# All expert score blocks from f32r parts, and 24 of them ahead of the combine loop instead of 14

## The chip, the cores and the metric

The kernel runs on one core of a Trainium2 chip. The metric is the time of one execution on the device in microseconds (us), from the profiler's first to its last event; of several runs the median counts. The engines are TensorE (PE, with its weight loads shown apart as PEld), VectorE (DVE), ScalarE (ACT), GpSimd (POOL) and SyncE (SP), which issues most of the DMAs. Each engine works through its own instructions in order.

## What is computed

The program is two layers of an encoder for 512 tokens of width 1024. A layer has two kinds of attention, an output projection with a LayerNorm, and then a retrieval over 16,384 single-neuron experts (PEER), which takes nearly all of the time spoken of here:

```python
def chunk(xc):
    q = (xc @ wq).reshape(PEER_CHUNK, PEER_HEADS, 2, half)
    sc = jnp.einsum('chpd,hpnd->chpn', q, sub_keys)
    ...
    eidx = jnp.take_along_axis(cidx, pos, axis=-1)
    g = jax.nn.softmax(top_s, axis=-1)
    u_sel = jnp.take(u, eidx, axis=0)
    a = jax.nn.gelu(jnp.einsum('chkd,cd->chk', u_sel, xc), approximate=False)
    w = (g * a).astype(x.dtype)
    v_sel = jnp.take(v, eidx, axis=0)
    return jnp.einsum('chk,chkd->cd', w, v_sel)
```

Each token picks 128 experts (8 heads of 16), takes the GELU of its product with their rows of `u`, weighs it with the gates `g`, and adds up their rows of `v`. Everything is in float32.

## The kernel before

The 512 tokens are four chunks of 128. Chunk 0 (`gat`) is done as the reference says it: its rows of `u` and `v` are gathered by indirect DMAs. Chunks 1 to 3 (`dense`, 384 tokens) are done densely: the 16,384 experts are 128 blocks (`NB`) of 128, all products of a block with the 384 tokens are computed, and the gates, which are zero for experts that a token did not pick, are laid out in a matrix `G` in DRAM.

A layer's retrieval runs through these stages, in the names of the code:

- `start(2)`, the queries and keys of chunk 0, with `top_pairs` and `gates` of chunk 3 beside it. `gates(c)` turns gates and expert indices of a chunk with TensorE and leaves them in flat tiles: `gh`, `glf`, `gl` (the gate's upper half, the rest, and the rest in f16) and `iT` (the two index halves).
- The tokens of the three dense chunks are turned by `transpose_rows` into `xTd`, a whole f32 copy; after the next stage two instructions (L908, L909) split it into `xTh` and `xTl`, its upper and lower part in the type f32r, on which TensorE multiplies at reduced precision.
- `spread()` builds `G` on chip, eight tokens at a time, 48 steps in all. A step has on DVE the one-hot masks `o12` (L873), the weighted masks `ah` (L874) and `al` (L875), on ACT two small instructions of `al` (L878) and two copies of the result into `stg` (L887), on TensorE 16 matmuls in f16 (L884, L885). Four steps fill a `stg` of 2 MB, which SP stores to `G`.
- `acts()` computes the expert blocks, `ge = gelu(u @ x)`. It is a generator, and a call `next(am)` makes one block. Of the first `LEAD` = 14 blocks each is 8 f32 matmuls on `xTd` (L826), which the hardware runs as two passes each. All later ones split the block's 1024 columns of `ut` into `uh` (ACT, L830) and `ul` (DVE, L831) and do 24 f32r matmuls (L833 to L835). During `spread()` one block is made every fourth step until there are 13; the 14th follows it.
- The combine loop runs over the 128 blocks. Iteration `blk` makes expert block `blk + LEAD`, splits a block of `v` into `vh`, `vl` (L1051, L1052), multiplies `ge` by the gates (`w`, L1055), splits that into `wh`, `wl` (L1058, L1059) and does 18 f32r matmuls of 512 columns (L1018 to L1020). Beside this, DVE does `jobs`, the 300 steps of chunk 0 (37 of ranking, 128 products with rows of `u`, 128 sums with rows of `v`, 7 at the end); 256 of them wait for a gather (L975) into one of four slots. The list `pace` says how the jobs are shared out: weight 4 for an iteration that still makes an expert block (`b < NB - LEAD`), 1 after that, 0 for the first and the last six.

A scheduler sets each engine's order from the program and a cost of its own. DVE in the combine loop is the exception (`manual_schedule`): there the order is that of the code. Pools lie in a stack on two sides of SBUF (`left`, `right`), so that a pool can only be made where an earlier one was released; `ws`, four buffers of 1 MB, holds `w_pq`, `ut` and `vt` in turn.

```python
        for i, _ in enumerate(spread()):
            if i % 4 == 0 and len(gel) < LEAD - 1:
                next(am)
        act.copy(xTh, xTd)
        v.tensor_tensor(out=xTl, in0=xTd, in1=xTh.bitcast(F32), op=SUB)
        while len(gel) < LEAD:
            next(am)
```

Of the kernel before, what the change touches and what calls it, by code (L numbers as in the profile page):

```python
# [34 lines left out]
GS = 2.0 ** 15  # L35
TG = 32
GB = 4
LEAD = 14
NTAIL = 6
NCAND = [TK // (a + 1) for a in range(TK)]  # L40
COFF = [sum(NCAND[:a]) for a in range(TK)]
# [4 lines left out]
def encoder_kernel(ctx: ExitStack, tc: tile.TileContext, x, ln_in_g, ln_in_b, w_in, qn_g, kn_g, sink,  # L46
# [18 lines left out]
    def sbuf(name, bufs=1, side="left"):  # L65
        return tc.alloc_tile_pool(name=name, bufs=bufs, side=side, reuse_waits="tile")
# [10 lines left out]
    h = cp.tile([P, NC, D], F32, name="h")  # L77
# [121 lines left out]
    for l in range(L):  # L199
        kp = sbuf(f"kp{l}", bufs=2, side="right")  # L200
# [86 lines left out]
        for c in gat + dense:  # L287
            cs = slice(c * P, (c + 1) * P)
# [7 lines left out]
            b = proj(c, wk, "ps_k")  # L296
# [470 lines left out]
        gp = sbuf(f"ge{l}")  # L767
        xp = sbuf(f"x{l}")
        lp = sbuf(f"lg{l}")
        xd = sbuf(f"xd{l}")  # L770
        ga = sbuf(f"ga{l}")
        flat = {}

        def gates(c):

            b = acc_bank("ps_t")
            i12 = ga.tile([P, 2, P], F32, tag="i12", name="i12", bufs=1)
            v.tensor_copy(i12[:, 0], i1f[:, c, :])
            v.tensor_copy(i12[:, 1], i2f[:, c, :])
            for i, src in enumerate((gte[:, c, :], i12[:, 0], i12[:, 1])):  # L780
                pe.transpose(b[:, i * P:(i + 1) * P], src, ident)
            gT = ga.tile([P, P], F32, tag="gT", name="gT", bufs=1)
            gh = ga.tile([P, P], F16, tag="gh", name="gh", bufs=3)
            glf = ga.tile([P, P], F32, tag="glf", name="glf", bufs=3)
            gl = ga.tile([P, P], F16, tag="gl", name="gl", bufs=3)
            iT = ga.tile([P, P // 8, 2, 8], F16, tag="iT", name="iT", bufs=3)
# [12 lines left out]
        gates(order[2])  # L799
        pt.release()  # L800
        tp.release()
        sp = sbuf(f"sp{l}", bufs=2, side="right")
        sp.tile([P, 8, P, 2], F16, tag="o12", name="o12")
        for tag in ("ah", "al"):
            sp.tile([P, 4, P, 2], F16, tag=tag, name=tag)
        xTd = xd.tile([P, KD, ND], F32, name="xTd")
        sp.tile([P, NB, TG], F32, tag="stg", name="stg", bufs=1)
        for ci, c in enumerate(dense):
            transpose_rows(h[:, c, :], xTd[:, :, ci * P:(ci + 1) * P], f"tr_x{c}")
        gg0 = xp.tile([P, NTG, GB, TG], F32, name="gg0")  # L810
        xTh = xp.tile([P, KD, ND], F32R, tag="xT", name="xTh", bufs=2)
        xTl = xp.tile([P, KD, ND], F32R, tag="xT", name="xTl", bufs=2)
        ff = "p k e -> p (k e)"
        gel = []

        def acts():

            for g2 in range(NB // 2):
                ut = load_w(peer_ut[l, g2], "ut")
                for bi in range(2):  # L820
                    us = ut[:, bi * D:(bi + 1) * D]
                    b = mm_bank("ps_a")
                    if len(gel) < LEAD:
                        u4 = us.rearrange("p (k e) -> p k e", k=KD)
                        for k in range(KD):
                            pe.matmul(b[:, :ND], u4[:, k, :], xTd[:, k, :], start=k == 0, stop=k == KD - 1)  # L826
                    else:
                        uh = up.tile([P, KD, P], F32R, tag="uh", name="uh")
                        ul = up.tile([P, KD, P], F32R, tag="ul", name="ul")
                        act.copy(uh.rearrange(ff), us)  # L830
                        v.tensor_tensor(out=ul.rearrange(ff), in0=us, in1=uh.rearrange(ff).bitcast(F32), op=SUB)  # L831
                        for k in range(KD):
                            pe.matmul(b[:, :ND], uh[:, k, :], xTh[:, k, :], start=k == 0, stop=False)  # L833
                            pe.matmul(b[:, :ND], uh[:, k, :], xTl[:, k, :], start=False, stop=False)  # L834
                            pe.matmul(b[:, :ND], ul[:, k, :], xTh[:, k, :], start=False, stop=k == KD - 1)  # L835
                    ge = gp.tile([P, ND], F32, tag="ge", name="ge", bufs=LEAD)
                    act.activation(ge, b[:, :ND], AF.Gelu)
                    gel.append(ge)
                    yield
# [62 lines left out]
                        keep(2 * GB, NB)  # L902

        am = acts()
        for i, _ in enumerate(spread()):
            if i % 4 == 0 and len(gel) < LEAD - 1:
                next(am)
        act.copy(xTh, xTd)  # L908
        v.tensor_tensor(out=xTl, in0=xTd, in1=xTh.bitcast(F32), op=SUB)  # L909
        while len(gel) < LEAD:  # L910
            next(am)


        ga.release()
        xd.release()
        sp.release()
        kp.release()
        up = sbuf(f"u{l}", bufs=2)
        ep = sbuf(f"ex{l}", bufs=2, side="right")
        ep.tile([P, D], F32R, tag="vh", name="vh")  # L920
        ep.tile([P, D], F32R, tag="vl", name="vl")
        ep.tile([P, NTG, TG], F32, tag="w", name="w")
        ep.tile([P, ND], F32R, tag="wh", name="wh")
        ep.tile([P, ND], F32R, tag="wl", name="wl")
        ep.tile([P, NTG, GB, TG], F32, tag="gg", name="gg")
# [100 lines left out]
        with tc.manual_schedule(engines={mybir.EngineType.DVE}):  # L1026
            for g2 in range(NB // 2):
                if g2 > 0:
                    load_v(g2)
                vt = vts[g2]  # L1030
                if g2 == 0:
                    gg = gg0
                elif (g2 * 2) % GB == 0:
                    gg = ep.tile([P, NTG, GB, TG], F32, tag="gg", name="gg")
                    load_g(gg, g2 * 2, 0, NTG)
                for bi in range(2):
                    blk = g2 * 2 + bi
                    if len(gel) < NB:
                        next(am)
                    turn = max(0, blk + LEAD - NB) % 3  # L1040
                    if turn == 1:
                        t = xp.tile([P, KD, ND], F32R, tag="xT", name="vwt", bufs=2).rearrange("p k n -> p (k n)")
                        vh, vl, wh, wl = t[:, :D], t[:, D:2 * D], t[:, 2 * D:2 * D + ND], t[:, 2 * D + ND:2 * (D + ND)]
                    else:
                        vp, tg_h, tg_l = (up, "uh", "ul") if turn else (ep, "vh", "vl")
                        vh = vp.tile([P, D], F32R, tag=tg_h, name="vh")
                        vl = vp.tile([P, D], F32R, tag=tg_l, name="vl")
                        wp, tg_h, tg_l, nb = (gp, "ge", "ge", LEAD) if turn else (ep, "wh", "wl", None)
                        wh = wp.tile([P, ND], F32R, tag=tg_h, name="wh", bufs=nb)
                        wl = wp.tile([P, ND], F32R, tag=tg_l, name="wl", bufs=nb)  # L1050
                    act.copy(vh, vt[:, bi, :])  # L1051
                    v.tensor_tensor(out=vl, in0=vt[:, bi, :], in1=vh.bitcast(F32), op=SUB)  # L1052
                    ge = gel[blk]
                    w_ = ep.tile([P, NTG, TG], F32, tag="w", name="w")
                    v.scalar_tensor_tensor(w_, gg[:, :, blk % GB, :], 1.0 / GS,  # L1055
                                           ge.rearrange("p (a t) -> p a t", a=NTG), op0=MUL, op1=MUL)
                    wf = w_.rearrange("p a t -> p (a t)")
                    act.copy(wh, wf)  # L1058
                    v.tensor_tensor(out=wl, in0=wf, in1=wh.bitcast(F32), op=SUB)  # L1059
                    if blk < NB - NTAIL:  # L1060
                        for c in dense:
                            for n in range(2):
                                combine(c, n, blk, wh, wl, vh, vl)
                    else:
                        parts.append((blk, wh, wl, vh, vl))
                    want = len(jobs) * sum(pace[:blk + 1]) // sum(pace)
                    while done < want:
                        f, j = jobs[done]
                        f(j)
                        done += 1  # L1070
# [81 lines left out]
```

## Time and profile before

| | |
|---|---|
| runs | 3059.69, 3058.49, 3059.13 us; median 3059.13 us |
| profiled execution | 3056.56 us, of which the span of the core's instructions is 3054.5 us |
| granted TensorE clock, mean | 0.996 of full speed |
| PE busy | 2980.2 us (98%) |
| DVE, ACT, POOL busy | 2420.0, 1333.8, 756.4 us |
| DMA | 749.44 MB, 245 GB/s in the mean |

The profile gives the busy time of each engine, its groups of instructions with what ended the idle time before them, the waits, the chain of work that ended last, and each instruction in order of time. The durations of matmuls are modelled and overlap; what a matmul costs is read from the distance of two starts. Below, layer 0 is read; layer 1 has the same stages about 1514 us later.

### The profile page before, as it was taken

Reading aid. Unit: us, or ns where it says so; the run is one execution under the profiler, and the core shown is the slowest. Engines: PE = TensorE matmul, PEld = TensorE weight load, DVE = VectorE, ACT = ScalarE, POOL = GpSimd, SP = SyncE. Lnnn points to the kernel's source line nnn. Section 1 sums busy time; section 2 is a strip of 40 time slices with the busy share of each in tenths; the row PEclk is TensorE's granted clock in tenths of the full one; section 3 lists DMA queues with packets and bytes.
Section 4 is the critical chain, followed back from the end, with each engine's and each line's share of the span. In section 5 each row is a group of like instructions: output and inputs, shape, how many; then the busy total and the mean of one; then the engine's idle time right before and its main releaser. Section 6 shows DMA issues by size and latency. Waiting matters only on the chain. (4 is left out here: it accounts for less than half of the span.)

```text
span 3054.5 us, 47487 instructions
## 1 busy us (share of the span) xinstructions
PE 2980.2 (98%) x17858; PEld 2696.5 (88%) x17858; DVE 2420.0 (79%) x5050; ACT 1333.8 (44%) x2646; POOL 756.4 (25%) x524
## 2 busy tenths in 40 slices
PE   7999999999999999999999999999999999999998
PEld 7999877999999999999898998779999999999997
DVE  7767998778777777877777779977788777777777
ACT  4664277343333333333347642764333333333332
POOL 0000000024434454454000000000344434455440
PEclk9999999999999999999999999999999999999999
DMA  5014767569889889889420247675698888988982
GB/s 195 27 58 148 242 241 289 194 226 332 324 306 327 320 302 332 313 310 327 165 97 15 72 150 268 247 297 174 248 330 306 321 325 304 325 322 304 327 312 90
DMA packets 262230, 749.44 MB, mean 245 GB/s; under 512 B 19952, under 2 KB 130288, under 8 KB 231792
## 3 DMA queue, kind: packets, MB, share of 16 engines
q1 hardware_dynamic: 188272, 477.94, 43.5%
q0 software_dynamic: 73728, 268.47, 24.5%
q8 instruction: 140, 2.29, 0.3%
q14 instruction: 90, 0.74, 0.1%
HBM read 691.81 MB, written 54.53 MB: 244 GB/s over the span
## 5 line engine op out<-in xcount | busy, mean ns | idle before, releaser
L975 POOL DMA_INDIRECT gt<-in_dram,idx x512 | 748.3, 1461 | 2042.5 <-DVE idx L966 1184.8
L833 PE MATMUL ps_a<-xTh,uh 128*128 128x384 f32 x1824 | 610.1, 334 | 3.7 <-ACT uh L830 3.7
L835 PE MATMUL ps_a<-xTh,ul 128*128 128x384 f32 x1824 | 610.1, 335 | 0.0
L834 PE MATMUL ps_a<-xTl,uh 128*128 128x384 f32 x1824 | 609.9, 334 | 0.0
L1020 PE MATMUL ff<-vh,wl 128*128 128x512 f32 x1476 | 575.8, 390 | 0.0
L1018 PE MATMUL ff<-vh,wh 128*128 128x512 f32 x1476 | 575.0, 390 | 0.1
L1019 PE MATMUL ff<-vl,wh 128*128 128x512 f32 x1476 | 573.8, 389 | 0.0
L1051 ACT CAST vh<-vt 128x1024 fp32r<-128x1024 f32 x246 | 258.1, 1050 | 608.5 <-PE ff L1020 308.2
L1052 DVE TENSOR_TENSOR vl<-vt,vh 128x1024 fp32r<-128x1024 f32 x246 | 301.1, 1224 | 195.3 <-ACT vh L1051 191.0
L833 PEld LDWEIGHTS ps_a<-xTh,uh 128*128 128x128 f32 x1824 | 342.5, 188 | 14.4 <-ACT uh L830 5.6
L834 PEld LDWEIGHTS ps_a<-xTl,uh 128*128 128x128 f32 x1824 | 342.4, 188 | 10.4
L981 DVE CUSTOM_DVE_ANT_0 junk<-gt,h 128x1024 bf16<-128x1024 f32 x256 | 313.1, 1223 | 38.2 <-DMA gt<-in_dram,idx 33.6
L835 PEld LDWEIGHTS ps_a<-xTh,ul 128*128 128x128 f32 x1824 | 342.4, 188 | 0.1
L1058 ACT CAST wh<-w 128x384 fp32r<-128x384 f32 x246 | 126.5, 514 | 477.5 <-DVE w L1055 473.5
L1020 PEld LDWEIGHTS ff<-vh,wl 128*128 128x128 f32 x1476 | 277.1, 188 | 58.2
L992 DVE SCALAR_TENSOR_TENSOR gacc<-gt,gw,gacc 128x1024 f32<-128x1024 f32 x252 | 311.6, 1280 | 20.5 <-DMA gt<-in_dram,idx 20.3
L1018 PEld LDWEIGHTS ff<-vh,wh 128*128 128x128 f32 x1476 | 276.9, 188 | 49.6 <-ACT wh L1058 0.9
L1019 PEld LDWEIGHTS ff<-vl,wh 128*128 128x128 f32 x1476 | 277.1, 188 | 48.8
L831 DVE TENSOR_TENSOR ul<-ut,uh 128x1024 fp32r<-128x1024 f32 x228 | 277.8, 1219 | 21.7 <-ACT uh L830 21.7
L830 ACT CAST uh<-ut 128x1024 fp32r<-128x1024 f32 x228 | 240.0, 1053 | 120.1 <-PE ps_a L834 118.7
L1059 DVE TENSOR_TENSOR wl<-w,wh 128x384 fp32r<-128x384 f32 x246 | 137.5, 559 | 157.3 <-ACT wh L1058 157.3
L826 PE MATMUL ps_a<-xTd,ut 128*128 128x384 f32 x448 | 156.1, 492 | 0.0
(291 smaller groups left out, 4836.4 us busy)
## 6 DMA issues: line engine op xcount, KB each, us to landing
ut<-in_dram SPq DMA_DIRECT2D x128, 1024.0 KB
vt<-in_dram SPq DMA_DIRECT2D x128, 1024.0 KB
w_pq<-in_dram SPq DMA_DIRECT2D x48, 1024.0 KB
gg<-G SPq DMA_DIRECT2D x62, 768.0 KB
G<-stg SPq DMA_DIRECT2D x24, 1920.0 KB
w_o<-in_dram SPq DMA_DIRECT2D x24, 1024.0 KB
w_q<-in_dram SPq DMA_DIRECT2D x8, 1024.0 KB
gt<-in_dram,idx POOLq DMA_INDIRECT x512
```

What stands on the lines that cost most here:

```text
L831: v.tensor_tensor(out=ul.rearrange(ff), in0=us, in1=uh.rearrange(ff).bitcast(F32), op=SUB)
L833: pe.matmul(b[:, :ND], uh[:, k, :], xTh[:, k, :], start=k == 0, stop=False)
L834: pe.matmul(b[:, :ND], uh[:, k, :], xTl[:, k, :], start=False, stop=False)
L835: pe.matmul(b[:, :ND], ul[:, k, :], xTh[:, k, :], start=False, stop=k == KD - 1)
L975: pool.indirect_dma_start(out=t, out_offset=None, in_=src, in_offset=bass.IndirectOffsetOnAxis(ap=idx[:, j:j + 1], axis=0))
L981: v.tensor_tensor_reduce(out=jk, in0=t, in1=h[:, c, :], op0=MUL, op1=ADD, scale=1.0, scalar=0.0, accum_out=a_[:, j:j + 1])
L992: v.scalar_tensor_tensor(acc[j % 2], t, w_[:, j:j + 1], acc[j % 2], op0=MUL, op1=ADD)
L1018: pe.matmul(b, wh[:, cs], vh[:, ns], start=blk == 0, stop=False)
L1019: pe.matmul(b, wh[:, cs], vl[:, ns], start=False, stop=False)
L1020: pe.matmul(b, wl[:, cs], vh[:, ns], start=False, stop=blk == NB - 1)
L1051: act.copy(vh, vt[:, bi, :])
L1052: v.tensor_tensor(out=vl, in0=vt[:, bi, :], in1=vh.bitcast(F32), op=SUB)
```

## The change

- All 128 expert blocks are made from f32r parts. The branch with f32 matmuls on `xTd` goes, and so do `xTd` and the two instructions that split it. `transpose_rows` writes `xTh` (ACT, L135) and `xTl` (DVE, L137) chunk half by chunk half, straight from PSUM.
- `LEAD` is 24. During `spread()` one block is made every second step until there are 21 (`LEAD - REST`); three follow it.
- The flat gates of a chunk lie in one tile `fl` from the ring of the activations `ge`, which has `LEAD` buffers; that is why three of the 24 blocks wait for the end of `spread()`.
- `up`, the pool of `uh` and `ul` with two buffers each, is made ahead of `spread()`, and `kp` is released before it.
- `LEAD` also moves the border in `pace`: weight 4 for `b < 104`, 1 for 104 to 121. The 300 jobs are the same.

```diff
-LEAD = 14
+LEAD = 24
+REST = 3
...
-            gh = ga.tile([P, P], F16, tag="gh", name="gh", bufs=3)
-            glf = ga.tile([P, P], F32, tag="glf", name="glf", bufs=3)
-            gl = ga.tile([P, P], F16, tag="gl", name="gl", bufs=3)
-            iT = ga.tile([P, P // 8, 2, 8], F16, tag="iT", name="iT", bufs=3)
+            fl = gp.tile([P, 3, P], F32, tag="ge", name="fl", bufs=LEAD)
+            glf = fl[:, 0]
+            gh, gl = (fl[:, 1].bitcast(F16)[:, i * P:(i + 1) * P] for i in range(2))
+            iT = fl[:, 2].bitcast(F16).rearrange("p (o a t) -> p o a t", a=2, t=8)
...
+        kp.release()
+        up = sbuf(f"u{l}", bufs=2)
+        for tag in ("uh", "ul"):
+            up.tile([P, KD, P], F32R, tag=tag, name=tag)
...
-        xTd = xd.tile([P, KD, ND], F32, name="xTd")
...
-            transpose_rows(h[:, c, :], xTd[:, :, ci * P:(ci + 1) * P], f"tr_x{c}")
+            cs = slice(ci * P, (ci + 1) * P)
+            transpose_rows(h[:, c, :], xTh[:, :, cs], f"tr_x{c}", lo=xTl[:, :, cs])
...
-                    if len(gel) < LEAD:
-                        u4 = us.rearrange("p (k e) -> p k e", k=KD)
-                        for k in range(KD):
-                            pe.matmul(b[:, :ND], u4[:, k, :], xTd[:, k, :], start=k == 0, stop=k == KD - 1)
-                    else:
-                        uh = up.tile([P, KD, P], F32R, tag="uh", name="uh")
...
+                    uh = up.tile([P, KD, P], F32R, tag="uh", name="uh")
...
         for i, _ in enumerate(spread()):
-            if i % 4 == 0 and len(gel) < LEAD - 1:
+            if i % 2 == 0 and len(gel) < LEAD - REST:
                 next(am)
-        act.copy(xTh, xTd)
-        v.tensor_tensor(out=xTl, in0=xTd, in1=xTh.bitcast(F32), op=SUB)
         while len(gel) < LEAD:
             next(am)
```

How the change moves instructions on DVE shows at two places. The first is the entry to `spread()` in layer 0; `t` and `i2f` end the ranking of chunk 3, `gT` is the first instruction of its gates after TensorE has turned them. Before:

```order
L564 TENSOR_TENSOR t_4663<-t_4663 128x256
L565 TENSOR_TENSOR i2f<-t_4663 128x128
L779 CAST i_4998<-i2f 128x128
L873 TENSOR_TENSOR o_5065<-iota_110,iT 128x2048
L873 TENSOR_TENSOR o_5106<-iota_110,iT 128x2048
L874 TENSOR_TENSOR ah<-o_5065,gh 128x1024
L875 TENSOR_TENSOR al<-o_5065,gl 128x768
L874 TENSOR_TENSOR ah<-o_5106,gh 128x1024
L787 TENSOR_SCALAR gT<-ps_t 128x128
```

Of the change, the end of the ranking, and then what stands ahead of the first masks:

```order
L637 TENSOR_TENSOR t_4651<-t_4651,ge 128x2048
L829 TENSOR_TENSOR ul<-ut,uh 128x1024
L565 TENSOR_TENSOR t_4651<-t_4651 128x1024
L829 TENSOR_TENSOR ul<-ut,uh 128x1024
L565 TENSOR_TENSOR t_4651<-t_4651 128x512
```

```order
L789 CAST fl<-fl 128x128
L137 TENSOR_TENSOR xTl<-tr_x_5017,xTh 128x4x128
L137 TENSOR_TENSOR xTl<-tr_x_5024,xTh 128x4x128
L137 TENSOR_TENSOR xTl<-tr_x_5031,xTh 128x4x128
L137 TENSOR_TENSOR xTl<-tr_x_5038,xTh 128x4x128
L137 TENSOR_TENSOR xTl<-tr_x_5045,xTh 128x4x128
L137 TENSOR_TENSOR xTl<-tr_x_5052,xTh 128x4x128
L871 TENSOR_TENSOR o_5061<-iota_110,fl 128x2048
L871 TENSOR_TENSOR o_5122<-iota_110,fl 128x2048
```

Two `ul` now stand inside the ranking, the gates of chunk 3 (`gT` to `fl`) and six `xTl` ahead of the first masks; before, the masks of the first two steps came ahead of `gT`.

The second place is the middle of `spread()`, two steps. Before:

```order
L873 TENSOR_TENSOR o_5232<-iota_110,iT 128x2048
L873 TENSOR_TENSOR o_5260<-iota_110,iT 128x2048
L874 TENSOR_TENSOR ah<-o_5232,gh 128x1024
L875 TENSOR_TENSOR al<-o_5232,gl 128x768
L874 TENSOR_TENSOR ah<-o_5260,gh 128x1024
L875 TENSOR_TENSOR al<-o_5260,gl 128x768
```

Of the change:

```order
L829 TENSOR_TENSOR ul<-ut,uh 128x1024
L871 TENSOR_TENSOR o_6733<-iota_110,fl 128x2048
L871 TENSOR_TENSOR o_6761<-iota_110,fl 128x2048
L872 TENSOR_TENSOR ah<-o_6733,fl 128x1024
L873 TENSOR_TENSOR al<-o_6733,fl 128x768
L872 TENSOR_TENSOR ah<-o_6761,fl 128x1024
L873 TENSOR_TENSOR al<-o_6761,fl 128x768
```

Every two steps one `ul` has come in. On TensorE the matmuls of two steps (32) are followed by half an f32 block before, and by a whole f32r block (24 matmuls) now.

## Rows read from the trace of the kernel before

**Rows 1.** Page of the profile: span and busy time of TensorE.
```profile
span 3054.5 us, 47487 instructions
...
PE 2980.2 (98%) x17858; PEld 2696.5 (88%) x17858; DVE 2420.0 (79%) x5050; ACT 1333.8 (44%) x2646; POOL 756.4 (25%) x524
```

**Rows 2.** Stages of layer 0: window, us, busy of the engines, PEclk, DMA share, GB/s.
```profile
409.00:531.00 122.00, 120.00 (x981) 85.62 (x978) 107.48 (x140) 96.41 (x209) 0.00 (x0) 1.00 0.68 260
...
560.00:1390.00 830.00, 830.00 (x4223) 758.16 (x4222) 650.81 (x944) 307.61 (x409) 343.69 (x237) 1.00 0.83 299
...
970.00:1390.00 420.00, 420.00 (x2138) 383.72 (x2138) 331.28 (x365) 152.31 (x206) 198.00 (x133) 1.00 0.88 316
1410.00:1460.00 50.00, 50.00 (x257) 45.73 (x256) 39.96 (x42) 17.96 (x25) 20.35 (x13) 1.00 0.89 324
```

**Rows 3.** TensorE in order of time, from the entry of spread to the first combine.
```profile
405.43 2.78 PE L129 MATMUL tr_x<-ident,h 128*128 128x128 f32 x24
408.05 0.22 PE L884 MATMUL ps_g<-ah,o 128*128 128x128 f16 x1
...
426.56 2.79 PE L826 MATMUL ps_a<-xTd,ut 128*128 128x384 f32 x8
429.19 0.22 PE L884 MATMUL ps_g<-ah,o 128*128 128x128 f16 x1
...
431.11 2.79 PE L826 MATMUL ps_a<-xTd,ut 128*128 128x384 f32 x8
...
530.65 0.44 PE L833 MATMUL ps_a<-xTh,uh 128*128 128x384 f32 x1 [1.51 <-ACT uh L830]
...
535.87 0.39 PE L1018 MATMUL ff<-vh,wh 128*128 128x512 f32 x1
```

**Rows 4.** TensorE in order of time, one iteration of the combine loop.
```profile
700.59 0.39 PE L1018 MATMUL ff<-vh,wh 128*128 128x512 f32 x1
...
704.68 0.34 PE L833 MATMUL ps_a<-xTh,uh 128*128 128x384 f32 x1
...
708.84 0.39 PE L1018 MATMUL ff<-vh,wh 128*128 128x512 f32 x1
```

**Rows 5.** DVE in order of time: two steps of spread, then ul and vl.
```profile
401.97 0.23 DVE L779 CAST i<-i2f 128x128 f32<-128x128 f16 x1
...
512.81 2.36 DVE L873 TENSOR_TENSOR o<-iota,iT 128x2048 f16<-128x2048 f16 x2
...
517.35 1.23 DVE L873 TENSOR_TENSOR o<-iota,iT 128x2048 f16<-128x2048 f16 x1
...
530.63 1.23 DVE L831 TENSOR_TENSOR ul<-ut,uh 128x1024 fp32r<-128x1024 f32 x1 [10.86 <-ACT uh L830]
531.77 1.22 DVE L1052 TENSOR_TENSOR vl<-vt,vh 128x1024 fp32r<-128x1024 f32 x1
```

**Rows 6.** ACT in order of time: copies of turned tokens, stg and uh.
```profile
406.81 2.56 ACT L134 COPY xTd<-tr_x 128x512 f32<-128x512 f32 x5
...
439.02 2.07 ACT L887 COPY stg<-ps_g 128x512 f32<-128x512 f32 x4 [1.04 <-PE ps_g L885]
440.97 0.74 ACT L878 ACTIVATE al<-o,glf 128x128 f16<-128x128 f16 x2
...
529.56 1.98 ACT L830 CAST uh<-ut 128x1024 fp32r<-128x1024 f32 x2
```

**Rows 7.** Instructions of line 136: the split of a turned half chunk.
```profile
L136 DVE TENSOR_TENSOR hTl<-tr_h,hTh x16: 637/685/692, 12.3 to 1555.8; 128x512 fp32r<-128x512 f32 x16
```

**Rows 8.** Waits 560 to 1390: for what, us in total, times, longest; gathers 970 to 1390.
```profile
DVE junk L981 <- DMA gt<-in_dram,idx: 16.2, 16, 5.0
DVE gacc L992 <- DMA gt<-in_dram,idx: 6.4, 7, 2.0
...
ACT uh L830 <- PE ps_a L834: 54.2, 91, 0.6
...
gt<-in_dram,idx POOLq DMA_INDIRECT x133
```

More of the change, by code (lines that the diff above doesn't have):

```diff
@@ L776, in gates @@
             b = acc_bank("ps_t")
-            i12 = ga.tile([P, 2, P], F32, tag="i12", name="i12", bufs=1)
+            i12 = pt.tile([P, 2, P], F32, tag="i12", name="i12", bufs=1)
             v.tensor_copy(i12[:, 0], i1f[:, c, :])
@@ L781, in gates @@
                 pe.transpose(b[:, i * P:(i + 1) * P], src, ident)
[L782 to L786 removed]
+            gT = pt.tile([P, P], F32, tag="gT", name="gT", bufs=1)
+            fl = gp.tile([P, 3, P], F32, tag="ge", name="fl", bufs=LEAD)
+            glf = fl[:, 0]
+            gh, gl = (fl[:, 1].bitcast(F16)[:, i * P:(i + 1) * P] for i in range(2))
+            iT = fl[:, 2].bitcast(F16).rearrange("p (o a t) -> p o a t", a=2, t=8)
             v.tensor_scalar(gT, b[:, :P], GS, None, op0=MUL)
@@ L805, in encoder_kernel @@
             sp.tile([P, 4, P, 2], F16, tag=tag, name=tag)
-        xTd = xd.tile([P, KD, ND], F32, name="xTd")
         sp.tile([P, NB, TG], F32, tag="stg", name="stg", bufs=1)
-        for ci, c in enumerate(dense):
-            transpose_rows(h[:, c, :], xTd[:, :, ci * P:(ci + 1) * P], f"tr_x{c}")
-        gg0 = xp.tile([P, NTG, GB, TG], F32, name="gg0")
+        gg0 = xp.tile([P, NTG, GB, TG], F32, tag="gg", name="gg", bufs=2)
         xTh = xp.tile([P, KD, ND], F32R, tag="xT", name="xTh", bufs=2)
         xTl = xp.tile([P, KD, ND], F32R, tag="xT", name="xTl", bufs=2)
+        for ci, c in enumerate(dense):
+            cs = slice(ci * P, (ci + 1) * P)
+            transpose_rows(h[:, c, :], xTh[:, :, cs], f"tr_x{c}", lo=xTl[:, :, cs])
         ff = "p k e -> p (k e)"
@@ L822, in acts @@
                     b = mm_bank("ps_a")
-                    if len(gel) < LEAD:
-                        u4 = us.rearrange("p (k e) -> p k e", k=KD)
-                        for k in range(KD):
-                            pe.matmul(b[:, :ND], u4[:, k, :], xTd[:, k, :], start=k == 0, stop=k == KD - 1)
-                    else:
-                        uh = up.tile([P, KD, P], F32R, tag="uh", name="uh")
[L829 to L835, printed above, removed]
+                    uh = up.tile([P, KD, P], F32R, tag="uh", name="uh")
+                    ul = up.tile([P, KD, P], F32R, tag="ul", name="ul")
+                    act.copy(uh.rearrange(ff), us)
+                    v.tensor_tensor(out=ul.rearrange(ff), in0=us, in1=uh.rearrange(ff).bitcast(F32), op=SUB)
+                    for k in range(KD):
+                        pe.matmul(b[:, :ND], uh[:, k, :], xTh[:, k, :], start=k == 0, stop=False)
+                        pe.matmul(b[:, :ND], uh[:, k, :], xTl[:, k, :], start=False, stop=False)
+                        pe.matmul(b[:, :ND], ul[:, k, :], xTh[:, k, :], start=False, stop=k == KD - 1)
                     ge = gp.tile([P, ND], F32, tag="ge", name="ge", bufs=LEAD)
@@ L904, in encoder_kernel @@
         am = acts()
+        for _ in range(0):
+            next(am)
         for i, _ in enumerate(spread()):
-            if i % 4 == 0 and len(gel) < LEAD - 1:
+            if i % 2 == 0 and len(gel) < LEAD - REST:
                 next(am)
-        act.copy(xTh, xTd)
-        v.tensor_tensor(out=xTl, in0=xTd, in1=xTh.bitcast(F32), op=SUB)
         while len(gel) < LEAD:
             next(am)
-        ga.release()
-        xd.release()
         sp.release()
-        kp.release()
-        up = sbuf(f"u{l}", bufs=2)
         ep = sbuf(f"ex{l}", bufs=2, side="right")
@@ L1033, in encoder_kernel @@
                 elif (g2 * 2) % GB == 0:
-                    gg = ep.tile([P, NTG, GB, TG], F32, tag="gg", name="gg")
+                    gg = xp.tile([P, NTG, GB, TG], F32, tag="gg", name="gg", bufs=2)
                     load_g(gg, g2 * 2, 0, NTG)
```

3 lines of the change are left out of this document (removed).

## The prediction

> **What bounds the kernel now.** I read the page first: TensorE is busy for 2980.2 of 3054.5 us [rows 1]. Busy matmuls overlap and prove little, so I went on to the stages [rows 2]. In the combine loop TensorE is covered without a gap (830.00 of 830, 50.00 of 50), and in the waits of this stage ACT's `uh` waits for TensorE, never for the DMA of `ut` [rows 8]: the engines behind it are early, and it sets the pace. In `spread()` it has 120.00 of 122 us, but DVE has 107.48 and ACT 96.41 [rows 2], so here a second bound is near.
>
> That stage has to be read in starts. Half an f32 block takes from 426.56 to 429.19, 2.63 us, so a block takes 5.26; the 32 matmuls of two spread steps take from 429.19 to 431.11, 1.92; the round is 4.55 [rows 3]. DVE's own round of two steps runs from 512.81 to 517.35, 4.54 [rows 5]. The two engines are level. In the loop an f32r block runs from 704.68 to 708.84, 4.16 us, and the 18 combine matmuls of an iteration from 700.59 to 704.68, 4.09 [rows 4]; an iteration is 8.25. So an expert block made from f32r parts is 1.10 us cheaper on TensorE than an f32 one, and the bound of the program is TensorE from 408 us to the end of a layer, if its neighbours keep up.
>
> **The change part by part, for one layer.**
>
> *The 14 f32 blocks become f32r blocks.* On TensorE 14 x (5.26 - 4.16) = **-15.4 us**. This row is the loop's, and the same instructions now run between f16 matmuls; I take it as it stands, since the granted clock is 1.00 in both stages [rows 2]. The Trainium skill would give more: its page "TensorE: Matmul & The Clock Gate", section "Back-to-back issue gap", has a gap of columns over 2.4 GHz plus 2.5 ns, 162.5 ns for 384 columns, so an estimated 3.90 us a block and 14 x 1.36 = -19.0 us; the trace has 4.16 us for 24 matmuls, 173 ns each, and the trace decides.
>
> *Ten more blocks ahead of the loop* cost 10 x 4.16 = 41.6 us there and save the same in the loop: 0 on TensorE.
>
> *The splits.* 21 blocks in `spread()` bring DVE 21 `ul` of 1.14 us each (530.63 to 531.77 [rows 5]) and ACT 21 `uh` of about 1.0 (1.98 for two [rows 6]). The new round of two steps and one block is then: TensorE 4.16 + 1.92 = 6.08 us; DVE 4.54 + 1.14 = 5.68; ACT four copies into `stg` 2.07, four `al` of 0.37 (two take 0.74), one `uh` 1.0 and one `ge` of 0.5 at most (a copy out of PSUM, its like, takes 0.51 here), 5.1 [rows 6]. All three fit, TensorE by 0.4. There are only two `uh` and `ul`, so each waits for the block two before it to leave TensorE, and one chain must fit as well: end of a block, `uh` and the step to `ul` 1.07 to 1.1 (529.56 to 530.63 [rows 5, 6]), `ul` 1.14, masks and weights of two steps 4.54, together about 6.9 with two handovers. The second half of the next two steps' matmuls is due on TensorE at 1.92 + 4.16 + 0.96 = 7.04. It fits by some 0.15 us: I cost the splits at **0**, covered by TensorE's own work. If that cover is gone, what DVE is late with comes on top in each of some 20 rounds (first rival).
>
> *The entry.* DVE does two `ul` (2.3 us) inside the ranking of chunk 3, whose last cast is at 401.97 [rows 5]; it moves to about 404.3, still ahead of the turning of the tokens at 405.43 [rows 3]. After this turning TensorE went on at once, at 408.05, with spread matmuls whose masks lay ready. Now the masks come after six `xTl`, so it can only go on with a block, and a block needs `xTh` and `xTl` of all three chunks. From 405.4: 0.7 until the first half chunk is in PSUM, 0.5 for ACT's copy (2.56 for five [rows 6]), then `xTl`, at most 0.685 each [rows 7]; the first four contraction slices need the fifth of them, so 405.4 + 1.2 + 5 x 0.6 = 409.6, or 409.0 if the turning starts earlier because ACT no longer has `al` ahead of the last query copy. I take 409.25: **+1.2 us**. Bounds: 0 if the turning moves up by 1.5 us, +4 if the early `uh` and `ul` hold up the queries of chunk 0 as well.
>
> *The whole copy* that goes (two large instructions after the first steps) lay beside TensorE's work: 0. The flat gates in `fl` are the same instructions: 0.
>
> *The entry to the combine loop.* Before, TensorE waited 1.51 us for the first `uh` [rows 3]; this `uh` now comes in the stream of the earlier ones. But the first combine still needs the last store of `G` and its load back, and three blocks cover that (some 9 us of matmuls behind the last spread step in the new order, against 8 before). In all, the stage before lost 535.87 - 408.05 = 127.8 less 14 x 5.26 + 24 x 1.92 + 26 f32r matmuls of 0.173 = 124.2, so 3.6 us. I leave the loss as it is: **0**, with -3.6 and +4 as its bounds.
>
> *The loop.* The jobs are spread with weights: before 300 x 4 / 460 = 2.61 an iteration, now 300 x 4 / 430 = 2.79, one of 0.52 MB each. The trace agrees with the first (133 gathers in 420 us are 2.61 in 8.25 us [rows 2, 8]). DVE's load grows by 0.18 x 1.2 = 0.2 us of 8.25, which is busy for 331.28 of 420 us now [rows 2]: hidden. DMA traffic grows from 316 GB/s by 0.095 MB an iteration to about 328 (second rival). At the end 24 iterations without an expert block, not 14, run at 4.09 us; in the 50 us window of that part TensorE has no gap at 324 GB/s [rows 2]. **0**.
>
> Sum of a layer: -15.4 + 1.2 = -14.2; two layers -28.4 us. The profiled execution took 3056.56 us, 2.6 less than the median of the three runs; the sum takes it to 3028.2, and the median of 3059.1 to **3030.7**.
>
> **The rivals.**
>
> *DVE and ACT set the pace of `spread()` (13%).* If ACT comes to `uh` only after the `al` of the next steps, DVE stands idle for one `uh`, and its round becomes 5.68 + 1.07 = 6.75, 0.67 over TensorE's. Over 20 rounds and two layers that is +27: about 3057, no change. Half of it gives 3044. For it: all three engines are within 1 us of each other in a round, and a level pair was already seen before. Against it: the chain fits as worked out, and before the change a round of 4.55 against DVE's 4.54 cost nothing. It decides once DVE idles over 0.4 us a round.
>
> *The gathers choke the loop (7%), the case on the other side.* They come 7% denser. If the DMA engines could not carry more than the 316 GB/s that they carry now, the 92 iterations with such jobs would take 8.25 x 328 / 316 = 8.56, +29 us a layer, and the program 3059 - 28 + 57 = 3088. At 322 GB/s it is half, 3059. For it: a DMA share of 0.88 [rows 2], and DVE, whose order is fixed, did wait for gathers, 22.6 us in 830 [rows 8]. Against it: the window at 324 GB/s ran without a gap on TensorE, and 316 at a share of 0.88 makes an estimated 359 at a full one. The Trainium skill, "DMA: Bandwidth & Descriptors", section "Bandwidth", puts a core's share of HBM at about 358 GB/s; by that rule 328 passes as well, and no run here shows the limit.
>
> *A block is cheaper, or less is lost, than I take it (8%).* By the columns of the combine (4.09 us for 18 matmuls of 512, so 0.170 for 384 [rows 4]) a block would take 4.09, another 0.07 x 28 = 2 us: 3029. If the loss of 3.6 us and the late entry go as well, a layer gains 5 more: 3019. Against it: the loss before came from waits that the change does not touch, and 4.16 is what the loop shows. By the skill's gap, above, the sum would be 2 x (-19.0 + 1.2), an estimated 3023.5.
>
> **How the numbers follow.** The forecast has 72%. A measurement of this kernel tells about 0.2% (6 us) from no change, so faster means under 3053. Faster: 72 + 8 + half of the first rival, 6 = 86%. Same: the rest of the first, 7%. Slower: 7%. The range takes the bounds of the entry and of the loss (-4 x 2 and +6 x 2 or so) and half of the first rival: 3018 to 3051.
>
> **What would show it.** After the change, 24 matmuls of a block in `spread()` should start 0.173 us apart and a round of two steps take 6.1 to 6.2 us; the first combine of layer 0 should start near 563 (408.05 + 127.8 + 1.2 - 15.4 + 41.6); from there to the same point of layer 1 the loop should be 41.6 us shorter, with no PE wait in it. TensorE's busy time should fall by some 31 us. Rounds of 6.5 us or more with DVE waiting for `uh` prove the first rival; iterations above 8.3 us with DVE waiting for gathers the second; a first block after 411 us would mean that the entry was priced too low.

## The result and the profile after

The changed kernel takes **3029.59 us** (median of four runs, 3028.57 to 3032.26); the kernel before took 3058.81 us beside it on the same chip. The ratio is 0.9906, 95% interval 0.9889 to 0.9923: 29 us less, where 28.4 were forecast. The profiled execution of the changed kernel has this page (span and busy times, as in [rows 1]):

```profile
span 3026.8 us, 48075 instructions
...
PE 2955.4 (98%) x18082; PEld 2726.0 (90%) x18082; DVE 2452.2 (81%) x5088; ACT 1345.5 (44%) x2672; POOL 744.3 (25%) x524
```

TensorE's busy time has fallen by 24.8 us and the span by 27.7; TensorE is as full as before. The stages of layer 0, in the columns of [rows 2]:

```profile
409.00:561.00 152.00, 151.93 (x1367) 145.70 (x1367) 135.96 (x169) 118.59 (x244) 0.00 (x0) 1.00 0.68 242
...
1000.00:1300.00 300.00, 300.00 (x1526) 273.92 (x1526) 245.77 (x268) 109.11 (x147) 149.75 (x102) 1.00 0.91 328
1370.00:1450.00 80.00, 80.00 (x383) 69.89 (x383) 65.67 (x75) 31.20 (x44) 29.11 (x18) 1.00 0.87 309
```

From 409 to 561 `spread()` is now covered by TensorE to 0.07 us (before, 120.00 of 122), with DVE at 89% of the stage. The loop moves 328 GB/s, as worked out, and TensorE has no gap in these stretches of it. TensorE in order of time, at the entry, in one round of two steps and a block, at the first combine, and at the last combine matmul of layer 0 (compare [rows 3]):

```profile
404.24 2.78 PE L130 MATMUL tr_x<-ident,h 128*128 128x128 f32 x24
407.64 0.61 PE L831 MATMUL ps_a<-xTh,uh 128*128 128x384 f32 x2 [0.61 <-ACT xTh L135]
408.80 0.45 PE L832 MATMUL ps_a<-xTl,uh 128*128 128x384 f32 x1 [0.55 <-DVE xTl L137]
...
459.40 0.42 PE L831 MATMUL ps_a<-xTh,uh 128*128 128x384 f32 x1
459.66 0.33 PE L832 MATMUL ps_a<-xTl,uh 128*128 128x384 f32 x1
459.83 0.34 PE L833 MATMUL ps_a<-xTh,ul 128*128 128x384 f32 x1
...
463.49 0.34 PE L833 MATMUL ps_a<-xTh,ul 128*128 128x384 f32 x1
465.49 0.42 PE L831 MATMUL ps_a<-xTh,uh 128*128 128x384 f32 x1
...
562.50 0.44 PE L831 MATMUL ps_a<-xTh,uh 128*128 128x384 f32 x1 [1.09 <-ACT ge L835]
562.77 0.33 PE L832 MATMUL ps_a<-xTl,uh 128*128 128x384 f32 x1
562.94 0.45 PE L1011 MATMUL ff<-vh,wh 128*128 128x512 f32 x1
...
1515.40 0.40 PE L1013 MATMUL ff<-vh,wl 128*128 128x512 f32 x1
```

The last combine matmul of layer 0 before the change:

```profile
1530.04 0.40 PE L1020 MATMUL ff<-vwt 128*128 128x512 f32 x1
```

A round runs from 459.40 to 465.49, 6.09 us: the block to 463.66 (the last start and 0.17), 4.26 us, and the 32 matmuls of two steps, left out between the last two rows of the round, 1.83 us. The first combine of layer 0 stands at 562.94; less the 41.6 us that the loop saves, that is 14.5 us earlier than the 535.87 of [rows 3]. The last one stands at 1515.40 against 1530.04, 14.6 us earlier: from the first combine to the last the layer takes 952.5 us where it took 994.2, 41.7 less. DVE in order of time, the end of the ranking, one round, and the first `w` of the combine loop (compare [rows 5]):

```profile
403.80 0.23 DVE L778 CAST i<-i2f 128x128 f32<-128x128 f16 x1
...
405.66 3.68 DVE L137 TENSOR_TENSOR xTl<-tr_x,xTh 128x512 fp32r<-128x512 f32 x6
...
464.77 1.23 DVE L829 TENSOR_TENSOR ul<-ut,uh 128x1024 fp32r<-128x1024 f32 x1 [0.46 <-ACT uh L828]
465.92 2.35 DVE L871 TENSOR_TENSOR o<-iota,fl 128x2048 f16<-128x2048 f16 x2
...
470.87 1.22 DVE L829 TENSOR_TENSOR ul<-ut,uh 128x1024 fp32r<-128x1024 f32 x1 [0.45 <-PE ps_g L883]
...
561.30 0.56 DVE L1048 SCALAR_TENSOR_TENSOR w<-gg,ge 128x384 f32<-128x384 f32 x1 [4.97 <-DMA gg<-G]
```

DVE's round is TensorE's, 6.10 us, with 0.45 us of it idle ahead of `ul`. That idle time is all that lies between this kernel and one in which DVE sets the pace of `spread()`.

### The profile page after: what moved, and what is told of

The parts are those of the page before. It is cut to its first block, busy times and chain, and to the rows that moved or that the text cites. A ratio compares the mean times of both kernels' runs of the same rounds, so it can differ in the third digit from the quotient of the medians.

```text
span 3026.8 us, 48075 instructions
## 1 busy us (share of the span) xinstructions
PE 2955.4 (98%) x18082; PEld 2726.0 (90%) x18082; DVE 2452.2 (81%) x5088; ACT 1345.5 (44%) x2672; POOL 744.3 (25%) x524
## 5 line engine op out<-in xcount | busy, mean ns | idle before, releaser
L831 PE MATMUL ps_a<-xTh,uh 128*128 128x384 f32 x2048 | 689.5, 337 | 3.3 <-ACT ge L835 2.1
L833 PE MATMUL ps_a<-xTh,ul 128*128 128x384 f32 x2048 | 686.9, 335 | 0.4 <-DVE ul L829 0.4
L832 PE MATMUL ps_a<-xTl,uh 128*128 128x384 f32 x2048 | 685.7, 335 | 1.1 <-DVE xTl L137 1.1
L1011 PE MATMUL ff<-vh,wh 128*128 128x512 f32 x1440 | 561.1, 390 | 0.0
L831 PEld LDWEIGHTS ps_a<-xTh,uh 128*128 128x128 f32 x2048 | 384.4, 188 | 12.5 <-ACT ge L835 2.7
L832 PEld LDWEIGHTS ps_a<-xTl,uh 128*128 128x128 f32 x2048 | 384.6, 188 | 11.1 <-DVE xTl L137 1.7
L833 PEld LDWEIGHTS ps_a<-xTh,ul 128*128 128x128 f32 x2048 | 384.4, 188 | 1.3 <-DVE ul L829 1.2
L828 ACT CAST uh<-ut 128x1024 fp32r<-128x1024 f32 x256 | 269.5, 1053 | 135.0 <-PE ps_a L832 126.0
L829 DVE TENSOR_TENSOR ul<-ut,uh 128x1024 fp32r<-128x1024 f32 x256 | 312.3, 1220 | 18.9 <-ACT uh L828 11.6
L1048 DVE SCALAR_TENSOR_TENSOR w<-gg,ge 128x384 f32<-128x384 f32 x256 | 141.4, 552 | 9.2 <-DMA gg<-G 9.2
## 6 DMA issues: line engine op xcount, KB each, us to landing
G<-stg SPq DMA_DIRECT2D x24, 1920.0 KB, 10.3
```

Source lines behind the costliest of these rows:

```text
L1011: pe.matmul(b, wh[:, cs], vh[:, ns], start=blk == 0, stop=False)
```

## The experiments

The theory: from about 408 us to the end of a layer TensorE is the bound; a block from f32r parts is cheaper there by about 1 us; and this reaches the time only because enough blocks lie beside the masks to keep TensorE busier than DVE. The rivals: the conversion alone does it, or the number of blocks ahead does; DVE has much room, or none; the gathers are near a limit.

| kernel | us, median | ratio to before, 95% interval |
|---|---|---|
| 14 f32r blocks ahead | 3075.68 | 1.0058 [1.0041, 1.0075] |
| 19 f32r blocks ahead | 3047.23 | 0.9963 [0.9949, 0.9977] |
| 20 f32 blocks ahead | 3080.19 | 1.0072 [1.0056, 1.0089] |
| 20 f32r blocks ahead | 3049.89 | 0.9970 [0.9959, 0.9982] |
| `ul` written twice in `spread()` | 3061.32 | 1.0014 [1.0003, 1.0024] |
| the change again | 3031.42 | 0.9912 [0.9899, 0.9926] |
| the change, pace border of before | 3079.05 | 1.0067 [1.0053, 1.0081] |
| jobs in 90 iterations | 3276.76 | 1.0716 [1.0699, 1.0732] |
| jobs in 98 iterations | 3208.64 | 1.0503 [1.0476, 1.0531] |
| 18 ahead, jobs in 90, four slots | 3300.74 | 1.0789 [1.0740, 1.0839] |
| 18 ahead, jobs in 90, six slots | 3061.93 | 1.0010 [0.9999, 1.0020] |
| early blocks spread evenly | 3032.87 | 0.9913 [0.9900, 0.9927] |

### The conversion without the number

```diff
-LEAD = 24
+LEAD = 14
...
-            if i % 2 == 0 and len(gel) < LEAD - REST:
+            if i % 4 == 0 and len(gel) < LEAD - REST:
```

> All blocks from f32r parts, but 14 ahead of the loop as before the change, one every fourth step of spread. My theory: TensorE would need 48 x 0.96 + 14 x 4.16 = 104 us from 409.3, but DVE needs 48 x 2.27 + 11 x 1.14 = 121.5 us for masks and splits, so DVE sets the pace of spread and its masks end near 531; the store of G and its load back put the first combine of layer 0 at 541 to 547, where it was 535.87 before the change. The loop is the one of before. Sum: 5 to 11 us more a layer, 3069 to 3081 us in all, slower than before the change. Rival (the conversion alone pays 1.10 us a block, the number ahead does nothing): first combine near 521, about 3030 us, as with 24 ahead.

It took 3075.68 us, 17 more than before the change, with the first combine at 541.4. So the conversion at 14 blocks, with the rest of the change as it is, loses. The waits of TensorE from 505 to 545 (line, releaser: us in total, times, longest) show why, and below them, in order of time, its last early matmul of a block, the wait after it, and the first combine:

```profile
PE ps_g L882 <- DVE ah L872: 8.9, 5, 2.0
PE ps_a L831 <- ACT ge L835: 4.7, 1, 4.7
```

```profile
511.10 0.34 PE L833 MATMUL ps_a<-xTh,ul 128*128 128x384 f32 x1
512.58 0.29 PE L882 MATMUL ps_g<-ah,o 128*128 128x128 f16 x2 [1.13 <-DVE ah L872]
...
541.37 0.71 PE L1011 MATMUL ff<-vh,wh 128*128 128x512 f32 x1
```

The code gives 11 blocks to `spread()` and three to its end, but the order that the scheduler made has all 14, and the loop's first, done on TensorE by 511, at step 38 of 48. From there on each pair of steps waits up to 2 us for DVE's masks. What TensorE has been relieved of, DVE has taken on, and DVE ends last.

### A number between

```diff
-LEAD = 24
+LEAD = 19
...
-            if i % 2 == 0 and len(gel) < LEAD - REST:
+            if i % 3 == 0 and len(gel) < LEAD - REST:
```

> 19 blocks ahead, one every third step of spread until there are 16. My theory: DVE needs 48 x 2.27 + 16 x 1.14 = 127 us, TensorE 125 us for all 19 blocks and 48 steps, and the three last blocks come after DVE's end, so DVE still sets the pace, by less: first combine of layer 0 at 544 to 552; less 5 x 4.16 = 20.8 that the loop saves, and against 535.87 before, 5 to 12 us gained a layer: 3035 to 3049 us, between before (3059) and the change (3030). Rival (the number ahead does nothing): 3030. Rival (each block ahead pays the same amount, a straight line from 14 to 24): halfway between the 14-block kernel and the change.

3047.23 us (ten runs from 3038 to 3060), first combine at 546.9, both inside the expectation and a little better than the straight line, which would give 3053. By the first combine a layer gains 9.8 us (535.9 + 20.8 - 546.9), so 19.6 were due and 11.6 came. In layer 0 the way from the first combine to the last, at 1527.62, takes 980.7 us where 994.2 - 20.8 = 973.4 were due; 4.1 of the 7.3 us are waits of TensorE for `wh` in the part of the loop without blocks, and the cause of the rest stays open.

### The number without the conversion, and the pair to it

The kernel before the change, with more blocks ahead:

```diff
-LEAD = 14
+LEAD = 20
...
-            if i % 4 == 0 and len(gel) < LEAD - 1:
+            if i % 2 == 0 and len(gel) < LEAD - 1:
```

> The kernel before the change, f32 blocks ahead as it was, but 20 of them instead of 14, one every second step until there are 19. My theory: TensorE sets the pace of spread (a round of two steps and a block 1.92 + 5.26 = 7.18 us, DVE 4.54), and each block moved ahead costs 5.26 there and saves 4.16 in the loop: 6 x 1.10 = 6.6 us lost a layer, about 3072 us (3068 to 3077). Rival (more blocks ahead pay by themselves, whatever they are made of, because they hide waits of spread or of the way to the loop): 3059 or less.

3080.19 us: more f32 blocks ahead lose, and by 21 us, not 13. In the middle of `spread()` the round is TensorE's, 7.05 us, and DVE waits for it (DVE in order of time):

```profile
465.80 2.36 DVE L873 TENSOR_TENSOR o<-iota,iT 128x2048 f16<-128x2048 f16 x2 [2.54 <-PE ps_g L885]
...
472.85 2.36 DVE L873 TENSOR_TENSOR o<-iota,iT 128x2048 f16<-128x2048 f16 x2 [2.55 <-PE ps_g L885]
```

That is the 7.18 of the expectation, a little cheaper. The first combine stands at 572.6, 11.7 us a layer late after the 25.0 that the loop saves, not 6.6. The difference is at the end, which the expectation had left out: on TensorE the blocks are used up at step 41 of 48, the last steps wait for masks (TensorE 5.0 us in three waits for `ah`), and one `ge` is waited for, 1.6 us.

The changed kernel with as many:

```diff
-LEAD = 24
+LEAD = 20
```

> The changed kernel with 20 blocks ahead, as many as the kernel with 20 f32 blocks ahead (3080 us, first combine of layer 0 at 572.6), so the conversion of the blocks is nearly all that lies between the two. My theory: 20 blocks cost 1.05 to 1.10 us less each on TensorE (21 to 22 us a layer), and DVE, with 48 x 2.27 + 17 x 1.14 = 128 us against TensorE's 46 + 83 = 129, does not take it back: first combine at 547 to 553, 3035 to 3045 us. It is then 4 x about 1.5 to 4 us a layer above the kernel with 24 ahead, because blocks missing beside the masks leave TensorE short of work at the end of spread. Rival (the conversion pays nothing at equal numbers ahead, the gain came from the number): 3070 to 3080.

3049.89 us: the conversion, with what goes with it, is worth 30.3 us at an equal number of blocks, and the rival is out. (The two kernels also differ in the entry and in where the flat gates lie; that the blocks are what pays is read from the rounds.) The forecast of 3035 to 3045 was missed by 5. Rounds of 6.09 against 7.05 us make 0.96 a block and 19.2 a layer; the first combine moved from 572.6 to 557.3, by 15.3. What is missing is mostly a wait of TensorE, on the way from the last block to the loop. One round, then this wait (line, releaser: us in total, times, longest):

```profile
497.52 0.42 PE L831 MATMUL ps_a<-xTh,uh 128*128 128x384 f32 x1
...
503.61 0.42 PE L831 MATMUL ps_a<-xTh,uh 128*128 128x384 f32 x1
```

```profile
PE ps_a L831 <- ACT ge L835: 7.4, 1, 7.4
```

On TensorE the 20 blocks and the loop's first are done by step 45, and DVE's last masks end alone (TensorE waits 1.6 us for `ah`). Then `ge` waits on ACT for `w`, and `w` on DVE 3.8 us for the load of `G`. With 24 blocks `w` waits even longer for `G`, 4.97 us, but TensorE has blocks left to do in that time and stands for 1.1 only. The 19 blocks of the run above, one every third step, reach to the end of the masks, and TensorE waits 1.5 us there: how the blocks are spaced counts beside their number.

### How much room DVE has

```diff
-                    v.tensor_tensor(out=ul.rearrange(ff), in0=us, in1=uh.rearrange(ff).bitcast(F32), op=SUB)
+                    for _ in range(2 if len(gel) < LEAD - REST else 1):
+                        v.tensor_tensor(out=ul.rearrange(ff), in0=us, in1=uh.rearrange(ff).bitcast(F32), op=SUB)
```

> The changed kernel, but the split ul of each of the 21 blocks made during spread is written twice on DVE (same values). My theory: a round of two steps and a block takes TensorE 6.10 us and DVE 5.65, so DVE has 0.45 us to spare; 1.14 more make it 6.8, 0.7 us over TensorE's round, in 20 rounds and two layers +28: 3050 to 3062 us, DVE without an idle gap in a round of 6.8. Rival (TensorE is the bound and DVE far off, the splits were free at any price): 3030. Rival (DVE sets the pace already, the whole of the added time shows): 21 x 1.14 x 2 = +48, 3077.

3061.32 us (ten runs from 3058 to 3071), 30 more than the change; 28 were expected. TensorE in order of time, its idle moments, and the window of seven rounds in the columns of [rows 2]:

```profile
506.11 0.44 PE L832 MATMUL ps_a<-xTh,uh 128*128 128x384 f32 x1 [0.41 <-ACT ge L836]
512.99 0.44 PE L832 MATMUL ps_a<-xTh,uh 128*128 128x384 f32 x1 [0.41 <-ACT ge L836]
519.86 0.44 PE L832 MATMUL ps_a<-xTh,uh 128*128 128x384 f32 x1 [0.41 <-ACT ge L836]
```

```profile
485.51:533.61 48.10, 45.20 (x393) 40.62 (x393) 47.52 (x57) 33.09 (x71) 0.00 (x0) 1.00 0.60 220
```

The round is 6.87 us. DVE is busy for 47.52 of 48.10 us and sets it; the `ge` that TensorE is released by is an instruction of ACT, which is busy for only 33.09. Of the 1.14 us added, 0.77 appear and the rest went into the idle time. One more instruction of this length in each round takes the whole gain: the margin that the forecast rested on was real and small.

### The border in `pace`

The next three runs leave `spread()` as it is. The first is the change itself, beside them:

> The changed kernel as it is, beside the next three on the same chip: 3027 to 3033 us by either theory.

It took 3031.42 us. Then with the border that the jobs had before:

```diff
-        pace = [0 if b < 1 or b >= NB - 6 else 4 if b < NB - LEAD else 1 for b in range(NB)]
+        pace = [0 if b < 1 or b >= NB - 6 else 4 if b < NB - 14 else 1 for b in range(NB)]
```

> The changed kernel with the jobs of the combine loop spread as before the change (weight 4 up to iteration 113, not 103: 2.61 an iteration, not 2.79). My theory: the gathers are hidden under TensorE at either density, so the time is that of the changed kernel within 3 us. Rival (the denser gathers already cost something in the loop): faster by up to 29 us a layer by the prediction's price, at least by more than 6 us in all.

3079.05 us, 47.6 **more**: both theories missed. The windows of the stretch in which blocks have run out, of the change and then of this kernel:

```profile
1420.00:1460.00 40.00, 40.00 (x177) 32.95 (x176) 33.22 (x42) 14.33 (x21) 1.68 (x1) 1.00 0.75 253
```

```profile
1420.00:1460.00 40.00, 30.79 (x117) 23.46 (x116) 30.98 (x34) 10.11 (x13) 22.57 (x15) 0.91 0.91 313
```

Iterations 104 to 113 make no block any more and last 4.09 us, but got 2.61 gathers each, as if they lasted 8.25. TensorE waits for `wh` in them, its granted clock falls to 0.91 in the mean (1.00 is its 2.4 GHz level; the lower one is 1.2 GHz), and the last combine matmul of layer 0 comes at 1537.95, 22.6 us late. Whether the bytes or the four slots of the next section hold these iterations up was not tested. The border that moved with `LEAD` is a part of the change without which the rest is lost. What the denser jobs cost in the long iterations can't be read from this run's time, but from a window before that border (that of the change stands above, with the profile after):

```profile
1000.00:1300.00 300.00, 300.00 (x1527) 274.00 (x1526) 235.79 (x269) 109.75 (x147) 142.91 (x94) 1.00 0.88 316
```

TensorE does 1527 matmuls here and 1526 in the change, without a gap in either, at 316 and 328 GB/s: in the long iterations the denser jobs of the change cost nothing, as the first theory had it.

### How dense the gathers may come

```diff
+        pace = [0 if b < 1 or b >= NB - 6 else 4 if b < 90 else 0 for b in range(NB)]
```

> The changed kernel with all jobs of chunk 0 in the first 90 iterations of the loop: 300 / 89 = 3.37 an iteration, 0.58 of 0.52 MB more than now, so 328 + 0.58 x 0.52 MB / 8.25 us = 365 GB/s if nothing slowed. My theory: the DMA engines carry an estimated 359 GB/s (316 at a share of 0.88), an iteration then takes 8.39 us and the two layers lose 2 x 89 x 0.14 = 25 us, 3045 to 3060 us, with DVE waiting for gathers and TensorE with gaps in the first 90 iterations. Rival (they carry 316 to 322): iterations of 9.35 to 9.5 us, 3200 us or more. Rival (no limit near): no change, 3030.

3276.76 us, as a limit near 320 GB/s would have it; but from 1000 to 1300 this kernel moves less than the change does:

```profile
1000.00:1300.00 300.00, 263.01 (x1224) 236.84 (x1222) 210.71 (x217) 85.05 (x117) 158.91 (x97) 0.93 0.82 294
```

294 GB/s at a DMA share of 0.82, against 328 at 0.91: not the bytes. The 1224 matmuls are 29.1 iterations of 10.3 us. In the waits of that stretch DVE, whose order is fixed, stands before a gather, and then TensorE before `ul`, which is queued behind it:

```profile
POOL gt L968 <- DVE gacc L985: 82.5, 34, 5.0
DVE gacc L985 <- DMA gt<-in_dram,idx: 61.3, 15, 6.1
...
PE ps_a L833 <- DVE ul L829: 35.2, 15, 5.9
```

GpSimd (POOL) issues a gather only when DVE has given a slot back. 97 gathers in 300 us on four slots are 12.4 us for a slot from one use to the next, 8.4 of them from issue to landing (median). This gave a second theory, the ring of slots, and three runs for it; the first two have the pace of the dense kernel and 18 blocks ahead, with six slots (this diff) and with four; the third has 24 blocks, four slots and the border 98.

```diff
-LEAD = 24
+LEAD = 18
...
+        more = ep.tile([P, 2, D], F32, tag="gt", name="gt", bufs=1)
...
-            return slots[:, used[0] % 4, :]
+            u = used[0] % 6
+            return slots[:, u, :] if u < 4 else more[:, u - 4, :]
```

> All jobs in the first 90 iterations as in the dense kernel (3.37 an iteration), but with six slots for the gathers instead of four, and 18 blocks ahead instead of 24, which makes the room for them. Theory after the dense kernel's run (iteration 10.3 us between 1000 and 1300, 294 GB/s, less than the 328 that the changed kernel moves): not the bytes are the limit but the ring of four slots, each of which is held from one use to its next for about 12 us (7.5 us landing, the rest waits and the issue). Six slots then give back nearly all: an iteration of 8.25 to 8.6 us at 350 GB/s or more, and 3050 to 3090 us. Rival (the bytes or the gathers themselves are at their limit): 10 us an iteration or more with six slots too, about 3290 us.

> The same with four slots, as a control of the 18 blocks ahead: iteration about 10.3 us between 1000 and 1300 by both theories, about 3300 us.

> The changed kernel with 24 blocks ahead, four slots and the jobs in the first 98 iterations, 300 / 97 = 3.09 an iteration, between the 2.79 of the change and the 3.37 of the dense kernel. Theory (a slot is held for about 12 us at least): 4 / 12 = 0.33 gathers a us, so 9.3 us an iteration, and with the rest of the loop free about 3130 to 3230 us. Rival (bytes, 347 GB/s of an estimated 359): no change, 3030 us.

With six slots 3061.93 us, with four and all else equal 3300.74, and 3208.64 at 3.09 jobs an iteration: all three times inside what the ring gives, though the iterations of 42 matmuls come out longer (at 3.09 jobs, by 1272 matmuls in 300 us, 9.9 us and not 9.3; in the control 10.6 and not 10.3). The window from 1000 to 1300 with six slots (and the one from 700 to 850), with four, and at 3.09:

```profile
1000.00:1300.00 300.00, 300.00 (x1528) 274.08 (x1527) 264.80 (x278) 108.05 (x147) 193.08 (x109) 1.00 0.94 346
700.00:850.00 150.00, 150.00 (x766) 137.20 (x765) 135.80 (x199) 55.01 (x74) 93.50 (x62) 1.00 1.00 371
```

```profile
1000.00:1300.00 300.00, 253.06 (x1184) 227.62 (x1184) 209.94 (x213) 84.13 (x117) 156.26 (x96) 0.92 0.81 287
```

```profile
1000.00:1300.00 300.00, 267.11 (x1272) 240.03 (x1271) 211.11 (x224) 83.97 (x121) 162.79 (x95) 0.95 0.82 295
```

Two more slots bring the iteration back to 8.25 us at 346 GB/s, and at 371 GB/s, with a DMA share of 1.00, TensorE still has no gap: the 359 estimated for a full share was too low. That the six-slot kernel is 30 us above the change comes from ahead of the loop, not from the gathers: its first combine stands at

```profile
553.25 0.71 PE L1013 MATMUL ff<-vh,wh 128*128 128x512 f32 x1
```

and with six blocks fewer ahead (6 x 4.16) it was due at 538.0 to match the change, so 15.3 us are lost a layer.

With four slots and the full pace, a slot would have 4 / 2.79 x 8.25 = 11.8 us in the changed kernel and 10.7 at 3.09 jobs. In the three kernels that choke it takes 12.4 to 12.6 (4 x 300 us over 97, 96 and 95 gathers). The changed kernel does not choke at 11.8, so these 12.4 to 12.6 are not a time that a slot needs in any case; DVE's own delays may be in them, which was not taken apart. The border lies somewhere between 2.79 and 3.09 jobs an iteration, and how near the change is to it no run shows. Its own waits for gathers in that stretch are still short:

```profile
DVE gacc L985 <- DMA gt<-in_dram,idx: 11.8, 18, 2.1
DVE junk L974 <- DMA gt<-in_dram,idx: 1.4, 2, 0.9
```

### Early blocks spread evenly

```diff
-            if i % 2 == 0 and len(gel) < LEAD - REST:
+            if len(gel) < min(LEAD - REST, 1 + i * (LEAD - REST) // 47):
```

> The changed kernel with its 21 early blocks spread evenly over the 48 steps of spread (21 in 47) and not one every second step until step 40. My theory: in the last seven steps DVE alone set the pace (2.27 us of masks a step against 0.96 on TensorE) and the last blocks were kept to fill this; TensorE hardly waits from 408.8 to the first combine, so even blocks give back 0 to 2 us a layer: 3026 to 3032 us. Rival (the uneven end costs more than the waits show): 6 us or more faster.

3032.87 us, the same as the change beside it. At 24 blocks TensorE is short of nothing in `spread()`, and a more even order of the blocks gives nothing back. No kernel of these beats the changed one.

## Why the prediction was right

- **The bound.** TensorE from 408 us on: confirmed by the windows, by the 20 f32 blocks that lose and by the pair at 20, where the conversion gives 30.3 us. The exception is the way to the loop: TensorE waits 1.09 us for `ge` there, and the first combine needs `w`, which waits 4.97 us for the load of `G`.
- **14 blocks at -1.10.** The size was slightly off in both halves: a block in `spread()` takes 4.26 us, not the 4.16 of the loop (its first start after f16 work is 0.26 from the next, not 0.17), and the 32 matmuls of two steps 1.83, not 1.92 (read from one pair of steps; the next pair before the change took 1.99). That the round of 6.09 is the 6.08 of the sum is because the two errors cancel, which nothing in the prediction foresaw. Starts within a block are 0.173 us apart as in the loop, so the shorter issue gap quoted from the Trainium skill ("TensorE: Matmul & The Clock Gate", "Back-to-back issue gap", 162.5 ns) isn't reached here either.
- **Ten more blocks cost nothing.** True of TensorE to about 1 us a layer (4.26 a block in `spread()`, 4.16 saved in the loop), but they are not neutral: they are what pays DVE's splits. With 14 f32r blocks the kernel is 17 us slower than before, with 24 it is 29 faster. The prediction had this only as "covered by TensorE's own work"; that was the step on which the sign hung.
- **The splits at 0.** Confirmed with the margin named: DVE idles 0.45 us a round, and 1.14 us more in each cost 30 us in all. The first rival's round of 6.75 us did not come about.
- **The entry at +1.2.** Mis-sized: the turning came 1.19 us earlier (404.24), two matmuls of the block ran ahead, and the third started at 408.80, so the block began in effect at 408.80 - 0.35 = 408.45, +0.4. The last cast of the ranking moved to 403.80, where 404.3 was forecast.
- **The loss ahead of the loop at 3.6.** 408.45 and 24 rounds of 6.09 and 26 matmuls of 0.173 make 559.1; the first combine came at 562.94, so 3.8. The place, 562.94, was forecast as 563.25. The size is right, but partly by chance: the 1.51 us for the first `uh` are gone, as forecast, and 1.09 us for `ge`, right behind the first `w`, have come in.
- **The loop at 0.** Right: 328 GB/s, and from the first combine to the last 41.7 us less, where 41.6 were forecast. The second rival had the right trigger and the wrong resource: it priced bytes, and with six slots 371 GB/s pass. The Trainium skill ("DMA: Bandwidth & Descriptors", "Bandwidth") gives about 358 GB/s as a core's share when both cores of a pair stream; this kernel on one core moved more, 371 GB/s from 700 to 850 with six slots. What chokes is the ring of four slots, from somewhere between 2.79 and 3.09 jobs an iteration on; at 3.09 it already costs 177 us. A chance of 7% was low for a border so near.
- **Busy time of TensorE.** It fell by 24.8 us, not 31. The sum let TensorE's idle time grow by 2.4 us, two late entries; it fell by 2.9 instead (74.3 to 71.4 us, span less busy time), and 24.8 + 2.9 is the 27.7 by which the span fell.
- **The range.** 3018 and 3051 do not follow from the bounds that are named: from 3030.7, -4 x 2 makes 3023, and +6 x 2 with half of the first rival 3056. The result lies in the middle, so nothing hangs on it.

## What to carry to other kernels

When a cheaper instruction on the bound engine brings work for its neighbour, count the neighbour's round too: here the gain existed only with enough blocks beside the masks to keep TensorE's round (6.10 us) above DVE's work in it (5.65). Where a ring of buffers feeds an engine in fixed order, compare the time that a slot has (slots by iteration over uses) with the time that it is held, not only bytes with bandwidth. A table of paces that follows a parameter belongs to the change: left at its old border it cost 48 us.

## What the runs showed of the hardware

- Denser gathers moved fewer bytes: with four slots 294 GB/s at 3.37 jobs an iteration against 328 at 2.79, since everything behind the waiting DVE slowed too, and TensorE's granted clock fell with its gaps, from 1.00 to 0.93 in the stretch.
- With six slots the same density ran at 371 GB/s and a DMA share of 1.00 from 700 to 850, and TensorE was covered for all 150 us: a DMA share of 1.00 did not yet delay it.
- A gather of 0.52 MB takes 7.5 us from issue to landing (median in the changed kernel from 1000 to 1300), while a slot goes 11.8 us from one use to the next there (4 x 300 us over 102 gathers); the rest is DVE's own step on the slot, the wait for its turn, and GpSimd's issue.
